# A hybrid mLSTM/attention layer: the second modulation's weight pieces, summed in the first piece's own buffer and loaded three ahead

## The chip, the cores and the metric

The kernel runs on 1 core of one Trainium2 chip. The metric is the device time of one execution in microseconds (us), the median of several runs. The engines are named as the profile names them: PE (TensorE; PEld are its weight loads), DVE (VectorE), ACT (ScalarE), POOL (GpSimd) and SP (SyncE). SP issues nearly all DMAs here, one after the other: a DMA that has to wait for something holds up those behind it in SP's queue.

## The reference

One layer over 1024 latent and 256 context tokens of width 1024. The part that the change touches is the modulation: a matrix product of the activated conditioning vector `c` with `w_ada`, whose six results shift, scale and gate the two halves of the layer.

```python
sh_a, sc_a, g_a, sh_f, sc_f, g_f = jnp.split(
    (jax.nn.silu(c) @ w_ada[l] + b_ada[l])[:, None, :], 6, axis=-1)
...
hx = modulate(rmsnorm(x, norm_mix[l]), sh_a, sc_a)
qm, km, vm, om, gates_x, qa, ka, va = project_tokens(hx, w_in[l], qk_conv_w[l], qk_conv_b[l], gate_b[l])
hm, _, _ = mlstm_bidirectional(qm, km, vm, gates_x, st_f, st_b, True)
...
x = x + g_a * (jnp.concatenate([y_m, y_a], axis=-1) @ w_out[l])
x = x + g_f * conv_glu(modulate(rmsnorm(x, norm_ffn[l]), sh_f, sc_f),
                       w_up[l], ffn_conv_w[l], ffn_conv_b[l], w_down[l])
return rmsnorm(x, final_norm)
```

`sh_a` and `sc_a` are needed at once (the first modulation). The other four, `g_a`, `sh_f`, `sc_f` and `g_f`, are needed only behind the mixer: they are the second modulation. `project_tokens` has four mLSTM heads and an attention part; `mlstm_bidirectional` runs a recurrence over chunks of tokens in both directions.

## The kernel before

The kernel is one long program. It norms and modulates the tokens, projects them head by head, runs the mLSTM heads and the attention, the output projection and the channel mixer. The loop that matters here is the one over the four mLSTM heads: in pass `h` the recurrence of head `h` (`mlstm(h, ...)`, about 30 steps, each up to a `yield`) runs beside the projections of head `h + 1` (`dense(h + 1, ...)`: L580 and L588 are products of keys and queries, L307 to L309 those of values and output gates). These passes are called head 0, 1 and 2 here, by `h`; in head 3 the attention's query projections (`qgen`) run beside the recurrence. After each step of the recurrence a budget (`RATE`) lets so much of the projections go. The engines' order in these passes is the order in which the code is written, for PE, DVE, ACT, POOL and SP alike (the manual schedule).

The second modulation is spread over heads 0 to 2 as a third strand, `ada_second`. Its matrix lies in DRAM as `w_ada2`, two halves of 32 pieces; a piece is 128 x 512 floats, 256 KB, and a tile of 2 KB in each partition. One call of the generator (`next(ada, 0)` behind nearly every step of the recurrence) does one piece: DVE multiplies it by a column of `silu(c)` (`c4`). The first piece of a half is written so into the accumulator `acc` (L830, a tensor_scalar), the 31 others are added to it (L832, a scalar_tensor_tensor). `total` (L816, L818) then sums over partitions on PE and adds the bias. For the first half `total` stands behind the fourth piece of the second half, for the second half at the end. The result `ada2` is transposed and goes to DRAM (`row_d`) through the tile `arw`, and is read again in the later stages.

The pieces lie in the pool `ap2`, opened with two buffers for each name: two tiles `w2` for pieces and two tiles `acc`. Two loads (L811) go out before the first piece; after piece `i` is used, piece `i + 2` is loaded, into the buffer that piece `i` leaves. The load is written behind the multiply-add that frees its buffer, so SP waits there for DVE.

Other names that the prediction uses: L152 loads a projection weight `wr` in two transfers of 512 KB, L156 (ACT) and L157 (DVE) split it into two parts. L549, L551, L554 and L556 are the short convolution and its activation on `kT`, by DVE, DVE, ACT and DVE. L600 and L601 copy a value block from PSUM to `va` and `ym` on ACT; PE's next block waits for that room. L690 is the backward state of the recurrence, L704 a gate on `ym`, L619 a copy of the context's values, L725 the decay matrix `ee` times scores, all on DVE. L722 are PE's scores, L736 PE's products with `ee`. L541 loads `tri`, a mask, L647 `ee`, L848 a block of attention keys `kb`.

Of the kernel before, what the change touches and what calls it, by code (L numbers as in the profile page):

```python
# [9 lines left out]
F32 = mybir.dt.float32  # L10
# [8 lines left out]
P = 128  # L19
# [59 lines left out]
def build(tc, I, out, dbg=None):  # L79
    nc = tc.nc  # L80
# [15 lines left out]
    def spc(n, i=0, w=1):  # L96
        a = SP[n][0] + i
        return sp[:, a:a + w]
# [45 lines left out]
    def load_split(src, w, rawf=None, split=True, alloc=True, now=range(2)):  # L144
        room = lambda: [st.tile([P, KT, XW], F32R, name=n, tag=n)[:].rearrange("p a b -> p (a b)")[:, :KT * w]
                        .rearrange("p (k f) -> p k f", k=KT) for n in ("wh", "wl")]
        hi, lo = room() if alloc else (None, None)
        raws = {}

        def load(q):  # L150
            raws[q] = rawf() if rawf else sr.tile([P, 4, XW], F32, name="wr", tag="wr")
            nc.sync.dma_start(raws[q][:, :, :w], src[:, 4 * q:4 * q + 4, :])  # L152

        def cut(q):
            ks, raw = slice(4 * q, 4 * q + 4), raws[q]
            S.copy(hi[:, ks, :w], raw[:, :, :w])  # L156
            V.tensor_tensor(out=lo[:, ks, :w], in0=raw[:, :, :w], in1=hi[:, ks, :w].bitcast(F32), op=ALU.subtract)  # L157

        if split:
            for q in range(2):  # L160
                load(q)
                cut(q)
            return hi, lo
        for q in now:
            load(q)

        def rest(qs=range(2)):
            nonlocal hi, lo
            if hi is None:
                hi, lo = room()  # L170
            for q in qs:
                cut(q)
            return hi, lo
        rest.load = load
        return rest
# [279 lines left out]
    qk = mstk.enter_context(tc.tile_pool(name="qk", bufs=2))  # L455
    tp = mstk.enter_context(tc.tile_pool(name="tp", bufs=2))
    astk = ExitStack()
    ap2 = astk.enter_context(tc.tile_pool(name="ap2", bufs=2))

    def g80(name, dt=F32):  # L460
        return gp.tile([P, 2, NCH, H], dt, name=name)
# [96 lines left out]
    def heads():  # L558
        return (qk.tile([P, NCH * P], F32, name="kT", tag="kT"), qk.tile([P, SEQ], F32, name="qT", tag="qT"),
                qk.tile([P, NCH, DH + 1], F32, name="va", tag="va"))  # L560
# [242 lines left out]
    def ada_second():  # L803
        R4 = 4 * KT
        pieces = [(n, r) for n in range(2) for r in range(R4)]
        tiles = {}

        def load(i):
            if i < len(pieces):
                tiles[i] = ap2.tile([P, 512], F32, name="w2", tag="w2")  # L810
                nc.sync.dma_start(tiles[i][:], I["w_ada2"][pieces[i]])  # L811

        def total(n, acc):
            pq = pl.tile([P, 512], F32, name="pq", tag="l")
            for j in range(4):
                T.matmul(pq[:, 4 * j:4 * j + 4], acc[:, j * P:(j + 1) * P], spc("c", 0, 4), start=True, stop=True)  # L816
            v = lambda a: a.rearrange("p (q j) -> p q j", q=4)
            V.tensor_tensor(out=v(ada2[:, 16 * n:16 * n + 16]), in0=pq[:, 0:16].rearrange("p (j q) -> p q j", q=4),  # L818
                            in1=v(spc("b2", 16 * n, 16)), op=ALU.add)

        load(0)
        load(1)
        yield
        prev = None
        for i, (n, r) in enumerate(pieces):
            w2 = tiles.pop(i)
            cr = spc("c4", r)
            if r == 0:
                acc = ap2.tile([P, 512], F32, name="acc", tag="acc")
                V.tensor_scalar(out=acc[:], in0=w2[:], scalar1=cr, scalar2=None, op0=ALU.mult)  # L830
            else:
                V.scalar_tensor_tensor(out=acc[:], in0=w2[:], scalar=cr, in1=acc[:], op0=ALU.mult, op1=ALU.add)  # L832
            load(i + 2)
            if r == 3 and n:
                total(n - 1, prev)
            prev = acc if r == R4 - 1 else prev
            yield
        yield
        yield
        total(1, prev)  # L840

    def row(i):
        return row_d[8 * i:8 * i + 8, :].rearrange("(o a) b -> o (a b)", o=1).broadcast_to([P, D])
# [90 lines left out]
    def qgen():  # L934
        for t, (i, b) in enumerate(qseq):
# [11 lines left out]
            if t == 2 * NL - 2:  # L947
                load_q(0)

    ada = ada_second()  # L950
    ahead_load = lambda h, i: load_split(I["w_h"][h, i] if h < H else I["w_q"][i], 256, split=False, alloc=False)

# [19 lines left out]
    for h in range(H):  # L972
        order_ = {mybir.EngineType.PE}
        if h + 1 < H:
            order_ |= {mybir.EngineType.DVE, mybir.EngineType.Activation, mybir.EngineType.Pool, mybir.EngineType.SP}
        else:
            wq = [wkq]
            late = lambda: wq.append(load_split(I["w_q"][1], 256, lambda: pq.tile([P, 4, 256], F32, name="wr", tag="rga")))
            for _ in ada:
                pass  # L980
            V.scalar_tensor_tensor(out=ada2[:, 16:24], in0=ada2[:, 16:24], scalar=1.0, in1=spc("nffn", 0, KT), op0=ALU.add, op1=ALU.mult)
            prw = pl.tile([P, 512], F32, name="prw", tag="l")
            T.transpose(prw[:32, 0:P], ada2[:], ident[:])
            arw = ap2.tile([P, 512], F32, name="arw", tag="w2")
            V.tensor_copy(arw[:32, 0:P], prw[:32, 0:P])
            nc.sync.dma_start(row_d[:], arw[:32, 0:P])
            cstk.close()
            astk.close()
            pq = rstk.enter_context(tc.tile_pool(name="pq", bufs=1, side="right"))
        wvo = []  # L990
        nh = heads() if h + 1 < H else None
        debt = 0.0
        with tc.manual_schedule(engines=order_):
            dn = dense(h + 1, wkq, wvo, *nh) if nh else qgen()
            rate = RATE if nh else RATE3
            for n, _ in enumerate(mlstm(h, *cur)):
                if nh is None and n == LW3:
                    late()
                    rga = pq.tile([P, D], F32, name="rga", tag="rga")
                    nc.sync.dma_start(rga[:], row(0))  # L1000
                if nh and n in (2, LW):
                    w = wnext((n // LW,))
                    if n == LW:
                        wvo.append(w)
                        wnext = ahead_load(h + 2, 0)
                elif nh and n in (24, 27):
                    wkq = wnext((n // 27,))
                    if n == 27 and h + 2 < H:
                        wnext = ahead_load(h + 2, 1)
                elif nh and n >= 3 and n != 15:  # L1010
                    next(ada, 0)
                debt += rate * (1 + (n == 0))
                while debt > 0:
                    w = next(dn, None)
                    if w is None:
                        break
                    debt -= w
            if nh is None:
                mstk.close()
                plk.close()  # L1020
                pl = pT = pa_.enter_context(tc.tile_pool(name="pT", bufs=2, space=PSUM))
                pO = pa_.enter_context(tc.tile_pool(name="pO", bufs=1, space=PSUM))
                pU = pa_.enter_context(tc.tile_pool(name="pU", bufs=1, space=PSUM))
                wm = rstk.enter_context(tc.tile_pool(name="wm", bufs=1, side="right"))
                kT2 = [wm.tile([P, KVH, NCH * P], F32R, name=f"kT2{i}") for i in range(2)]
                vv = wm.tile([P, NCH, KVH, P], F32R, name="vv")
                S.activation(vv[:, 0, 0, 0:1], eps_t[:], AF.Exp)
                kgens += [kprep(c) for c in range(NCH)]
                loads += [lambda: load_vv(0), lambda: load_vv(1)]
                wosteps += WOS  # L1030
            for _ in dn:
                pass
        cur = nh
# [23 lines left out]
    class Wout:  # L1057
# [8 lines left out]
        def load(self):  # L1066
            b = self.b
            self.xb = t3.tile([P, D], F32, name="x2", tag="x2") if self.attn else x2t()
            if self.attn:
                xs[b] = self.xb[:]  # L1070
            nc.sync.dma_start(self.xb[:], x2_d[b][:] if self.attn else I["x"][b * P:(b + 1) * P, :])
# [196 lines left out]
    for t in range(n + 2):  # L1268
# [3 lines left out]
        if t in WOT:  # L1272
            k = 4 + WOT.index(t)
# [215 lines left out]
    for i, b in enumerate(order):  # L1489
        prev = order[i - 1] if i else None  # L1490
# [71 lines left out]
    f = ExitStack()  # L1562
# [20 lines left out]
    def wsplit_h(R, n):  # L1583
# [5 lines left out]
        def lo():  # L1589
# [41 lines left out]
                                                                    tag={"a": "a", "f": "b", "b": "b"}.get(n, "c"))  # L1631
# [383 lines left out]
    for t, (p, ps, fresh) in enumerate(products):  # L2015
        for j in range(NP):
# [12 lines left out]
            if n - 1 in sums:  # L2029
                k = sums[n - 1]  # L2030
                m = len(PAIRS[k])
                add(V, b11[k][:, 0:m], b22[k][:, 0:m], b11[k][:, 0:m])
            if n + 2 in raws:
                q, k = steps[n + 2]
# [10 lines left out]
            if n in sums:  # L2045
                k = sums[n]
# [125 lines left out]
```

## Time and profile before

| what | value |
|---|---|
| median of 3 runs | 1273.13 us (1272.91 to 1273.3) |
| the profiled execution | 1274.79 us |
| its span in the profile | 1273.0 us |
| granted TensorE clock, mean | 0.997 |
| loads of pieces (L811) | 64, of 256 KB each, 81.6 to 305.6 us |
| multiply-adds into `acc` (L832) | 62, 746 ns median |
| head 0, 1, 2 begin with L580 at | 125.77, 190.85 and 257.93 us |

The span is shorter than the time of the execution by what lies around it. An engine's busy time is the time in which one of its instructions ran. In the list of waits an engine's idle time is put down to the instruction that ended it; SPq is SP's queue of DMAs. In the timeline an instruction's idle time before it stands in brackets, with what ended it, and neighbours of one line are merged (x2 are two).

### The profile page before, as it was taken

What the parts mean: (1) busy time and instruction counts of PE and PEld (TensorE: products, weight loads), DVE (VectorE), ACT (ScalarE), POOL (GpSimd) and SP (SyncE); (2) the same over time, 40 slices, a digit from 0 to 9 for tenths busy, and PEclk for the clock granted to TensorE, in tenths of its full rate; (3) what the DMA queues carried; (4) which work ended last, traced back from release to release, by engine and by line L of the source; (5) the groups of instructions that cost most, each with busy time, mean ns of one, the idle gap of its engine ahead of it and who ended that gap; (6) DMA issues with size and microseconds to landing.
All of it is one profiled execution on the core that took longest, in us unless ns stands there. A gap on an engine that the chain in (4) does not pass through costs nothing.

```text
span 1273.0 us, 19254 instructions
## 1 busy us (share of the span) xinstructions
PE 1238.7 (97%) x7047; PEld 1062.6 (83%) x7047; DVE 974.5 (77%) x1691; ACT 638.0 (50%) x1309; POOL 188.0 (15%) x162
## 2 busy tenths in 40 slices
PE   6999999999999999999999999999999999999997
PEld 4799998989898888887877888888888888788886
DVE  4873687868787888788987877777777776867887
ACT  6732556464765877775844333333333333434435
POOL 1200000000000443221002331232231232001000
PEclk9999999999999999999999999999999999999999
DMA  9541544453255333104413322333322337975553
GB/s 356 186 125 35 142 129 145 117 170 92 79 166 171 133 117 117 51 33 136 146 50 116 115 100 92 108 108 108 108 99 91 108 119 268 342 255 179 196 194 135
DMA packets 90560, 176.17 MB, mean 138 GB/s; under 512 B 12954, under 2 KB 29538, under 8 KB 90466
## 3 DMA queue, kind: packets, MB, share of 16 engines
q1 hardware_dynamic: 90178, 174.15, 40.6%
q8 instruction: 56, 0.92, 0.3%
q10 hardware_dynamic: 288, 0.79, 0.2%
q14 instruction: 38, 0.31, 0.1%
HBM read 136.58 MB, written 38.33 MB: 137 GB/s over the span
## 4 chain that ended last, share of the span: by engine, by line
PE 76%; DVE 9%; ACT 6%; DMA 5%; issue 2%; POOL 1%; SPq 0%; ACTq 0%; DVEq 0%; POOLq 0%
PE pd L2009 14%; PE pa L1471 8%; PE pc L1471 8%; PE pp L588 7%; PE pe L1471 4%; PE pd L1471 4%; PE pb L1471 4%; PE u L1177 3%; PE pt L1154 2%; PE pv L307 2%; PE pv L309 2%; PE pv L308 2%; PE po L307 1%; PE po L309 1%; PE po L308 1%
## 5 line engine op out<-in xcount | busy, mean ns | idle before, releaser
L1587 ACT CAST wh<-Rb 128x1024 fp32r<-128x1024 f32 (+1 forms) x63 | 56.8, 904 | 144.4 <-PE pd L1471 77.3
L2009 PE MATMUL pd<-dh,al 128*128 128x512 f32 x296 | 115.4, 390 | 0.9 <-DVE al L1352 0.9
L2009 PE MATMUL pd<-dl,ah 128*128 128x512 f32 x296 | 115.3, 389 | 0.0
L2009 PE MATMUL pd<-dh,ah 128*128 128x512 f32 x296 | 115.1, 389 | 0.0
L1471 PE MATMUL pc<-hB,wh 128*128 128x512 f32 x344 | 105.6, 389 | 0.0
L1471 PE MATMUL pa<-hB,wh 128*128 128x512 f32 x336 | 103.7, 390 | 0.3 <-ACT sn L1668 0.2
L1193 DVE TENSOR_TENSOR wl<-Rb,wh 128x1024 fp32r<-128x1024 f32 (+1 forms) x63 | 65.8, 1046 | 39.2 <-ACT wh L1587 38.7
L1704 POOL TENSOR_TENSOR tt<-vt,tt 128x512 f32<-128x512 f32 x22 | 29.6, 1343 | 368.5 <-ACT tt L1698 368.5
L588 PE MATMUL pp<-hl,wh 128*128 128x512 f32 x256 | 79.3, 405 | 0.0
L307 PE MATMUL pv<-wh,hl 128*128 128x256 f32 x256 | 76.1, 297 | 0.8 <-ACT ym L601 0.8
L1471 PEld LDWEIGHTS pc<-hB,wh 128*128 128x128 f32 x344 | 64.6, 188 | 13.4
L1471 PEld LDWEIGHTS pa<-hB,wh 128*128 128x128 f32 x336 | 62.9, 188 | 14.1 <-ACT sn L1668 1.1
L309 PE MATMUL pv<-wh,hl 128*128 128x256 f32 x256 | 72.3, 283 | 0.0
L308 PE MATMUL pv<-wl,hl 128*128 128x256 f32 x256 | 72.3, 282 | 0.0
L2009 PEld LDWEIGHTS pd<-dh,al 128*128 128x128 f32 x296 | 55.6, 188 | 13.2 <-DVE al L1352 1.6
L1471 PE MATMUL pc<-hB,wl 128*128 128x512 f32 x172 | 66.4, 389 | 0.0
L1471 PE MATMUL pa<-hB,wl 128*128 128x512 f32 x168 | 65.4, 389 | 0.0
L2009 PEld LDWEIGHTS pd<-dl,ah 128*128 128x128 f32 x296 | 55.6, 188 | 11.7 <-DVE dl L1352 0.3
L2009 PEld LDWEIGHTS pd<-dh,ah 128*128 128x128 f32 x296 | 55.6, 188 | 11.6
L1161 ACT CAST ph<-pt 128x512 fp32r<-128x512 f32 (+1 forms) x88 | 46.2, 525 | 28.2 <-PE pt L1154 28.0
L1471 PE MATMUL pb<-hB,wh 128*128 128x512 f32 x176 | 54.0, 390 | 0.6 <-ACT hB L1443 0.6
L1131 DVE TENSOR_REDUCE nm<-sps 128x1 f32<-128x641 f32 (+1 forms) x64 | 50.3, 786 | 4.9 <-PE sps L1127 3.5
(1080 smaller groups left out, 3702.9 us busy)
## 6 DMA issues: line engine op xcount, KB each, us to landing
w<-in_w_ada_dram SPq DMA_DIRECT2D x64, 256.0 KB, 2.7
br<-in_w_down_dram SPq DMA_DIRECT2D x25, 512.0 KB, 5.2
ar<-act_s SPq DMA_DIRECT2D x44, 256.0 KB, 3.1
Ra<-in_w_up_dram SPq DMA_DIRECT2D x21, 512.0 KB, 3.6
Rb<-in_w_up_dram SPq DMA_DIRECT2D x21, 512.0 KB, 3.6
act_a<-tt SPq DMA_DIRECT2D x33, 256.0 KB, 2.0
act_s<-tt SPq DMA_DIRECT2D x33, 256.0 KB, 2.0
wr<-in_w_h_dram SPq DMA_DIRECT2D x16, 512.0 KB, 4.4
```

The source lines that it names most:

```text
L307: T.matmul(ps, st_hi, mv_hi, start=first, stop=False)
L308: T.matmul(ps, st_hi, mv_lo, start=False, stop=False)
L309: T.matmul(ps, st_lo, mv_hi, start=False, stop=last)
L588: T.matmul(pp[:, 512 * n:512 * n + 512], wkq[sw][:, kt, cs], hl[n][part][:, kt, :], start=kt == 0 and sw + part == 0, stop=kt == KT - 1 an ...
L1131: V.tensor_reduce(out=self.nm[:, j:j + 1], in_=self.sv[j], axis=AX.X, op=ALU.max, negate=True)
L1161: S.copy(self.ph[i][:, :w], self.pt[i][:, :w])
L1177: T.matmul(self.u[:], vv[:, c, self.g], part[i][:, kk * 2 * P:(kk + 1) * 2 * P], start=kb + m == 0, stop=kb == last and m == 1)
L1193: sub = lambda e, o, x, y: e.tensor_tensor(out=o, in0=x, in1=y, op=ALU.subtract)
L1471: T.matmul(ps[:, cols], wt[sw][:, j, kt * P:kt * P + P], hB[part][:, blk, kt, cols], start=first and n == 0, stop=last and n == len(seq) - ...
L1587: S.copy(wt[0][:], src)
L1704: G.tensor_tensor(out=self.tt[:, h2_], in0=self.vt[:], in1=self.tt[:, h2_], op=ALU.mult)
L2009: T.matmul(ps[:], ac[sa][:, js], w[sw], start=first and n == 0, stop=last and n == 2, skip_group_check=not fresh)
```

## The change

The pool `ap2` has one buffer for each name, and there are four names, `w20` to `w23`: four tiles as before, of the same size, but any of them can take a piece. A list `rooms` says which are free. Four loads go out before the first piece. The first piece of a half is multiplied in its own tile, which then is the accumulator of that half; it isn't given back until the half is summed. Every other piece gives its tile back when it has been added. So three tiles take pieces while one half is in work, and the load that follows a multiply-add is the piece three steps ahead. At the turn of the halves both accumulators hold a tile, and two take pieces until `total` of the first half has read its accumulator; its tile is then given back, and the load into it waits for PE. `arw` uses the name `w20`.

```diff
-    ap2 = astk.enter_context(tc.tile_pool(name="ap2", bufs=2))
+    ap2 = astk.enter_context(tc.tile_pool(name="ap2", bufs=1))
...
-        tiles = {}
-
-        def load(i):
-            if i < len(pieces):
-                tiles[i] = ap2.tile([P, 512], F32, name="w2", tag="w2")
-                nc.sync.dma_start(tiles[i][:], I["w_ada2"][pieces[i]])
+        tiles, rooms = {}, list(range(4))
+
+        def load():
+            while rooms and todo_:
+                k, i = rooms.pop(0), todo_.pop(0)
+                tiles[i] = k, ap2.tile([P, 512], F32, name="w2", tag=f"w2{k}")
+                nc.sync.dma_start(tiles[i][1][:], I["w_ada2"][pieces[i]])
+
+        todo_ = list(range(len(pieces)))
...
-        load(0)
-        load(1)
+        load()
         yield
         prev = None
         for i, (n, r) in enumerate(pieces):
-            w2 = tiles.pop(i)
+            k, w2 = tiles.pop(i)
             cr = spc("c4", r)
             if r == 0:
-                acc = ap2.tile([P, 512], F32, name="acc", tag="acc")
+                acc, held_ = w2, k
                 V.tensor_scalar(out=acc[:], in0=w2[:], scalar1=cr, scalar2=None, op0=ALU.mult)
             else:
                 V.scalar_tensor_tensor(out=acc[:], in0=w2[:], scalar=cr, in1=acc[:], op0=ALU.mult, op1=ALU.add)
-            load(i + 2)
+                rooms.append(k)
             if r == 3 and n:
                 total(n - 1, prev)
-            prev = acc if r == R4 - 1 else prev
+                rooms.append(done)
+            load()
+            if r == R4 - 1:
+                prev, done = acc, held_
             yield
...
-            arw = ap2.tile([P, 512], F32, name="arw", tag="w2")
+            arw = ap2.tile([P, 512], F32, name="arw", tag="w20")
```

On PE, DVE, ACT and POOL every instruction keeps its place; on SP only loads of pieces move. In the changed program L811 is L812, L816 is L819, L830 and L832 are L832 and L834, and what stands behind is 5 lines further down. The names of tiles carry a number; `w_1427` is the first piece's tile.

The start of SP's queue, ahead of head 0 and at its first steps (line, what is written from where, shape, times). Before:

```order
L811 DMA w_1427<-in_w_ada_dram 128x512
L811 DMA w_1429<-in_w_ada_dram 128x512
L541 DMA tri<-in_cst_dram 128x256
L152 DMA wr<-in_w_h_dram 128x4x256 x2
L539 DMA m_d<-rr 40x256
L647 DMA ee<-m_d 128x2x256 x3
L811 DMA w_1563<-in_w_ada_dram 128x512
L647 DMA ee<-m_d 128x2x256
L811 DMA w_1582<-in_w_ada_dram 128x512
L152 DMA wr<-in_w_h_dram 128x4x256 x2
```

With the change:

```order
L812 DMA w_1427<-in_w_ada_dram 128x512
L812 DMA w_1429<-in_w_ada_dram 128x512
L812 DMA w_1431<-in_w_ada_dram 128x512
L812 DMA w_1433<-in_w_ada_dram 128x512
L541 DMA tri<-in_cst_dram 128x256
L152 DMA wr<-in_w_h_dram 128x4x256 x2
L539 DMA m_d<-rr 40x256
L647 DMA ee<-m_d 128x2x256 x4
L812 DMA w_1583<-in_w_ada_dram 128x512
L152 DMA wr<-in_w_h_dram 128x4x256 x2
```

Two loads have moved to the front, and the load of the first step is gone, since the first piece keeps its tile.

SP's queue in head 2, about the weights that are loaded for the attention's queries. Before:

```order
L811 DMA w_3125<-in_w_ada_dram 128x512
L647 DMA ee<-m_d 128x2x256
L811 DMA w_3145<-in_w_ada_dram 128x512
L152 DMA wr<-in_w_q_dram 128x4x256 x2
L811 DMA w_3193<-in_w_ada_dram 128x512
L811 DMA w_3212<-in_w_ada_dram 128x512
L848 DMA kb<-kv_d 128x2x64 x2
```

With the change:

```order
L812 DMA w_3125<-in_w_ada_dram 128x512
L647 DMA ee<-m_d 128x2x256
L812 DMA w_3145<-in_w_ada_dram 128x512
L152 DMA wr<-in_w_q_dram 128x4x256 x2
L812 DMA w_3193<-in_w_ada_dram 128x512
L812 DMA w_3212<-in_w_ada_dram 128x512
L853 DMA kb<-kv_d 128x2x64 x2
```

The rows stand alike; what has changed is which step of DVE reads which of these tiles. DVE's order at the same place, before:

```order
L832 SCALAR_TENSOR_TENSOR acc<-w_3145,sp,acc 128x512
L605 MEMSET va 128x10
L690 SCALAR_TENSOR_TENSOR cbk<-cbk,gd,pn 128x129
L787 SCALAR_TENSOR_TENSOR ym<-hid,hss,ym 128x128
L663 TENSOR_TENSOR ee<-ee,tri 128x256
L832 SCALAR_TENSOR_TENSOR acc<-w_3193,sp,acc 128x512
L549 SCALAR_TENSOR_TENSOR kT<-pp,sp,kT 128x1023
L551 SCALAR_TENSOR_TENSOR kT<-pp,sp,kT 128x1023
```

With the change (`w_2505` is the tile of the second half's first piece):

```order
L834 SCALAR_TENSOR_TENSOR w_2505<-w_3125,sp,w_2505 128x512
L605 MEMSET va 128x10
L690 SCALAR_TENSOR_TENSOR cbk<-cbk,gd,pn 128x129
L787 SCALAR_TENSOR_TENSOR ym<-hid,hss,ym 128x128
L663 TENSOR_TENSOR ee<-ee,tri 128x256
L834 SCALAR_TENSOR_TENSOR w_2505<-w_3145,sp,w_2505 128x512
L549 SCALAR_TENSOR_TENSOR kT<-pp,sp,kT 128x1023
L551 SCALAR_TENSOR_TENSOR kT<-pp,sp,kT 128x1023
```

The step ahead of L549 reads the tile that is loaded ahead of `wr` (w_3145), where before it read the one loaded behind it (w_3193).

## Prediction

> **What bounds the kernel now.** I read the profile's page first, then the waits, then the chain of waits and the timeline in the stretch where the pieces are used (126 to 326 us), and last the busy time by windows.
>
> ```profile
> span 1273.0 us, 19254 instructions
> ...
> PE 1238.7 (97%) x7047; PEld 1062.6 (83%) x7047; DVE 974.5 (77%) x1691; ACT 638.0 (50%) x1309; POOL 188.0 (15%) x162
> ...
> PE 76%; DVE 9%; ACT 6%; DMA 5%; issue 2%; POOL 1%; SPq 0%; ACTq 0%; DVEq 0%; POOLq 0%
> ```
>
> PE is busy for 97% of the span. So a wait on another engine has a price only where PE runs out of work because of it. The pieces are read by DVE, and DVE's waits for them are these (the waits of the stretch 90 to 330: who waits, for whom, sum in us, times, longest):
>
> ```profile
> DVE acc L832 <- DMA w<-in_w_ada_dram: 8.7, 6, 2.9
> ...
> DVE acc L830 <- DMA w<-in_w_ada_dram: 1.5, 1, 1.5
> ...
> PE pv L307 <- ACT ym L601: 0.8, 2, 0.6
> ...
> PE pn L710 <- DVE cbk L690: 0.7, 1, 0.7
> ```
>
> DVE stands still 8.7 + 1.5 = 10.2 us in 7 waits for a piece. That is not the price: in the same stretch PE waits for ACT and DVE only 0.8 + 0.7 us. What PE loses in all is found by comparing like with like. The heads 0, 1 and 2 run the same PE work behind each other, and the chain of waits shows the same two landmarks in each: the context product L580 that opens a head's projections, and the first L588 group behind the first use of `ee` (start us, us, what). L816 is PE's sum of a finished half, which head 0 hasn't.
>
> ```profile
> 125.77 2.88 PE pc__1491 L580 x24
> 157.81 1.39 PE pp L588 x6
> ...
> 190.85 2.88 PE pc__2263 L580 x24
> 224.02 1.38 PE pp L588 x6
> 229.49 0.79 PE pq L816 x8
> 257.93 2.88 PE pc__3051 L580 x24
> 292.50 1.38 PE pp L588 x6
> ```
>
> From landmark to landmark: head 0 takes 157.81 - 125.77 = 32.04 us, head 1 224.02 - 190.85 = 33.17, head 2 292.50 - 257.93 = 34.57. Head 1 loses 1.13 us and head 2 2.53 us, **3.66 us** together; L816 lies behind the landmark. Which of the seven waits is behind them is read from DVE's and ACT's timeline (start, us, engine, line; in brackets the idle time before and what ended it):
>
> ```profile
> 211.91 0.75 DVE L832 SCALAR_TENSOR_TENSOR acc<-w,sp,acc 128x512 f32<-128x512 f32 x1 [1.49 <-DMA w<-in_w_ada_dram]
> 215.26 1.03 ACT L554 ACTIVATE pp<-kT 128x1024 f32<-128x1024 f32 x1 [3.44 <-DVE kT L551]
> ...
> 280.38 0.75 DVE L832 SCALAR_TENSOR_TENSOR acc<-w,sp,acc 128x512 f32<-128x512 f32 x1 [2.86 <-DMA w<-in_w_ada_dram]
> 283.56 0.34 DVE L690 SCALAR_TENSOR_TENSOR cbk<-cbk,gd,pn 128x129 f32<-128x129 f32 x1
> 283.74 1.03 ACT L554 ACTIVATE pp<-kT 128x1024 f32<-128x1024 f32 x1 [4.79 <-DVE kT L551]
> ```
>
> One wait in each of the two heads, 1.49 and 2.86 us, stands just ahead of the convolution (L549, L551). ACT waits for L551 and copies `ym` (L601) only after it; PE waits for that copy, and in head 2 for L690 too. The other waits fall in head 0 or behind the second landmark, where PE has work queued.
>
> **The change part by part.** *The wait that goes.* Why these two pieces come late is in SP's timeline; first one row of head 1, then head 2, and behind them the landing times of all 64 loads of pieces:
>
> ```profile
> 203.94 0.34 SPq L811 DMA_DIRECT2D w<-in_w_ada_dram  x1
> ...
> 271.04 0.34 SPq L811 DMA_DIRECT2D w<-in_w_ada_dram  x1
> 271.43 2.25 SPq L152 DMA_DIRECT2D wr<-in_w_q_dram  x2
> ...
> 274.83 2.19 SPq L811 DMA_DIRECT2D w<-in_w_ada_dram  x2
> ```
>
> ```profile
> DMA to landing us min/median/max: 2.4/2.7/5.5
> ```
>
> A piece is issued when the piece two steps before it has been used. The late one (w_3193) was issued at 274.83, behind two halves of the next weights (`wr`, 512 KB each), and landed just ahead of its use at 280.38: some 5.5 us, the longest of all 64, against a median of 2.7. In the changed program the queue stands the same, but the load ahead of `wr` is already the one that this step reads. Issued at 271.04 and landed 2.4 to 5.5 us later, it is there by 273.4 to 276.5; DVE is ready for it at 280.38 - 2.86 = 277.52. So even the slowest landing seen leaves 1.0 us, and the wait goes whole. In head 1 the load ahead of such a pair goes out at 203.94, is there by 209.4 at the latest, and DVE is ready at 211.91 - 1.49 = 210.42.
>
> *What is late next.* The piece behind `wr` is now read one step later, at L832 behind L704. Before, that step stood at 285.55; without the wait it stands at 282.69:
>
> ```profile
> 285.55 0.75 DVE L832 SCALAR_TENSOR_TENSOR acc<-w,sp,acc 128x512 f32<-128x512 f32 x1
> ```
>
> The piece issued at 274.83 landed by 280.38, so 2.3 us are left. And DVE, so freed, stands where it stood in head 0, which cost PE nothing. Two of its instructions in the three heads, L704 and the copy L619 for which PE's L722 waits:
>
> ```profile
> 149.59 1.22 DVE L704 SCALAR_TENSOR_TENSOR ym<-ym,rw 128x1024 f32<-128x1024 f32 x1
> 153.78 0.41 DVE L619 COPY va<-pt 128x256 f32<-128x256 f32 x1
> ...
> 215.94 1.22 DVE L704 SCALAR_TENSOR_TENSOR ym<-ym,rw 128x1024 f32<-128x1024 f32 x1
> 220.39 0.41 DVE L619 COPY va<-pt 128x256 f32<-128x256 f32 x1
> ...
> 284.42 1.22 DVE L704 SCALAR_TENSOR_TENSOR ym<-ym,rw 128x1024 f32<-128x1024 f32 x1
> 288.87 0.41 DVE L619 COPY va<-pt 128x256 f32<-128x256 f32 x1
> ```
>
> Counted from each head's L580, L704 stands at 23.82, 25.09 and 26.49 us; less the waits 23.82, 23.60 and 23.63. L619 stands at 28.01, 29.54 and 30.94; less the waits 28.01, 28.05 and 28.08. So heads 1 and 2 come to head 0's schedule within 0.1 us, and I take the whole difference of PE: 1.13 + 2.53 = 3.66 us.
>
> *How PE's loss is counted.* The windows show idle PE directly (stretch, length, PE busy first):
>
> ```profile
> 190.60:257.60 67.00, 66.67 (x474) 61.67 (x473) 51.51 (x124) 37.05 (x105) 0.00 (x0) 1.00 0.46 138
> 257.60:326.00 68.40, 66.96 (x473) 61.70 (x473) 49.17 (x120) 37.26 (x106) 0.00 (x0) 1.00 0.37 110
> ```
>
> By them PE is idle 67.00 - 66.67 = 0.33 and 68.40 - 66.96 = 1.44 us, 1.77 together, half of 3.66. I take 3.66: start times of the same work are measured, while a record that overlaps the next covers part of a stall. The Trainium skill, Perfetto Trace Analysis, Identifying the Most-Contended Engine, says that matmul busy time is a poor measure of what is left in PE, because of pipelining; by that rule the 1.77 is a floor. The granted clock in these rows is 1.00, so no slower clock is in either sum.
>
> *What the change adds.* Two more loads go out at the start, behind the two at 81.56:
>
> ```profile
> 81.56 0.91 SPq L811 DMA_DIRECT2D w<-in_w_ada_dram  x2
> 93.06 0.33 SPq L541 DMA_DIRECT2D tri<-in_cst_dram  x1
> ```
>
> They take another 0.91 us of SP's queue, in which nothing is issued from 82.5 to 93.06; the cost is nothing, and without that cover it would be 0.91 us of a queue whose next DMA waits for PE anyway. The first piece of a half is scaled in place. That form isn't in the trace; its neighbours are the same form into another tile (484 ns) and the in-place multiply-add (746 ns):
>
> ```profile
> L832 DVE SCALAR_TENSOR_TENSOR acc<-w,sp,acc x62: 730/746/753, 136.2 to 309.0; 128x512 f32<-128x512 f32 x62
> L830 DVE TENSOR_SCALAR acc<-w,sp x2: 479/484/489, 134.8 to 224.8; 128x512 f32<-128x512 f32 x2
> ```
>
> I take 484; at worst it is 2 x 0.27 = 0.54 us of DVE, at two places where PE doesn't wait for it. At the turn of the halves both accumulators hold a buffer, and for two steps loads run two ahead as before. Then the load into the first accumulator's buffer waits for L816 on PE, and SP's queue behind it with it. PE began L816 at 229.49, ahead of the multiply-add at 230.67 that frees the other buffer of that step; I take nothing.
>
> ```profile
> 230.67 0.73 DVE L832 SCALAR_TENSOR_TENSOR acc<-w,sp,acc 128x512 f32<-128x512 f32 x1
> ...
> 237.22 0.74 DVE L832 SCALAR_TENSOR_TENSOR acc<-w,sp,acc 128x512 f32<-128x512 f32 x1
> ```
>
> **The sum.** The profiled execution took 1274.79 us (span 1273.0, and 1.79 around it): 1274.79 - 3.66 = 1271.13. It lies 1.66 above the median of the runs, 1273.13. The median less the same 3.66 is **1269.5 us**.
>
> **The rivals.** *Only the idle rows count* (1.77 us): 1273.13 - 1.77 = 1271.4. For it: nothing else in PE's rows is idle. Against it: the landmarks.
>
> *The wait moves one step.* If the piece behind `wr` lands after 282.69, 2.3 us later than it did, DVE waits there instead, ahead of the same L619 and L722. If head 2 keeps its loss and only head 1 is healed, the gain is 1.13: 1272.0. For it: the pair still stands in front. The Trainium skill, DMA: Bandwidth & Descriptors, Queues, rings and completion order, says that each DMA engine takes the descriptors of a ring in order; by that rule the late landing stays and only its reader moves. The trace agrees as far as the 5.5 us of that piece go.
>
> *Given back later, or the change doesn't do what it says.* PE comes 3.66 us earlier into the rest, and something that doesn't move with it (a landing, another engine) takes it back: 1273.1. Against it: from 292 us on every transfer is issued behind work that moves along.
>
> *Slower: the load that waits for L816 holds SP.* The piece that it brings is read at 237.22 and needs 2.7 us, so SP must be free by 234.5, 4.2 us after L816's end at 230.28. A longer hold delays DVE one for one, and beyond the 0.3 us that a wait had free (2.86 - 2.53) PE too; the gain is used up from a hold of 4.2 + 0.3 + 3.66 = 8.2 us on. If SP were held as long as its longest wait for DVE in this stretch,
>
> ```profile
> SPq L152 <- DVE wl L157: 20.6, 1, 20.6
> ```
>
> PE would lose 20.6 - 4.5 = 16.1 us, less the gain 12.4: 1285.6. Against it: L816 is in PE's order at a fixed place, ahead of what frees the other buffer.
>
> **How the numbers follow.** A measurement of this kernel tells about 0.2% from no change, 2.55 us: faster means below 1270.6. Forecast 1269.5: 0.70, its own range 1268.7 to 1270.4 (all of 3.66 and some of head 3's waits, or 0.9 less). Idle rows 1271.4: 0.08. Wait moved 1272.0: 0.08. Given back 1273.1: 0.10. Slower: 0.04. Up to 1272.0 the cases hold 0.86, so the range is 1268.7 to 1272.0. Faster 0.70, same 0.08 + 0.08 + 0.10 = 0.26, slower 0.04.
>
> **What would show it.** In the changed profile DVE's waits for `w` should be almost gone (below 1 us of 10.2), the landmarks 32.0 to 32.2 us apart in all three heads, PE's waits for L601 and L690 gone, and the rest behind 292 us as long as before. The forecast is wrong if DVE waits at the step behind L704, if SP waits for PE at L816's load, or if the landmarks close up and the span doesn't.

## The result and the profile after

The changed kernel takes 1269.11 us (median of 7 runs, 1268.51 to 1271.46), the kernel before in the same comparison 1273.13 us (7 runs, 1271.55 to 1274.38): a ratio of 0.9976, 95% interval 0.9967 to 0.9985 (the quotient of the two medians is a little lower, 0.9968). A second comparison, below, gave 0.9969 (0.9956 to 0.9981). The change is worth 3 to 4 us.

The profiled execution of the changed kernel took 1268.82 us. The head of its page, and the chain that ended last:

```profile
span 1267.0 us, 19250 instructions
...
PE 1234.5 (97%) x7047; PEld 1059.8 (84%) x7047; DVE 974.1 (77%) x1691; ACT 639.0 (50%) x1309; POOL 187.7 (15%) x162
...
PE 80%; DVE 7%; ACT 5%; DMA 4%; issue 2%; SPq 1%; POOL 1%; ACTq 0%; DVEq 0%; POOLq 0%
```

PE bounds it as before, with a larger part of the chain. From the waits of the stretch 90 to 330 us (who waits, for whom, sum in us, times, longest):

```profile
ACT pp L554 <- DVE kT L551: 5.4, 4, 1.9
...
DVE w L834 <- DMA w<-in_w_ada_dram: 0.8, 3, 0.4
...
PE pn L680 <- ACT kwf L659: 0.2, 1, 0.2
```

DVE's waits for pieces have gone from 10.2 us in 7 to 0.8 us in 3. PE's waits for L601 and L690 are gone; what is left to PE up to 326 us, where the prediction counted 0.8 + 0.7 us, is 0.2 us. In the chain of waits the two landmarks of each head now read (start us, us, what):

```profile
125.27 2.88 PE pc__1495 L580 x24
...
157.30 1.39 PE pp L588 x6
...
190.34 2.88 PE pc__2264 L580 x24
...
222.35 1.38 PE pp L588 x6
...
256.28 2.88 PE pc__3051 L580 x24
...
288.33 1.39 PE pp L588 x6
```

The distances are 32.03, 32.01 and 32.05 us; before they were 32.04, 33.17 and 34.57. Heads 1 and 2 now take what head 0 took, to within 0.02 us.

The same place in head 2, by SP's timeline and then DVE's:

```profile
269.39 0.35 SPq L812 DMA_DIRECT2D w<-in_w_ada_dram  x1
269.78 2.26 SPq L152 DMA_DIRECT2D wr<-in_w_q_dram  x2
273.19 2.19 SPq L812 DMA_DIRECT2D w<-in_w_ada_dram  x2
```

```profile
275.79 0.75 DVE L834 SCALAR_TENSOR_TENSOR w<-w,sp,w 128x512 f32<-128x512 f32 x1
276.45 1.29 DVE L549 SCALAR_TENSOR_TENSOR kT<-pp,sp,kT 128x1023 f32<-128x1023 f32 x1
277.77 1.28 DVE L551 SCALAR_TENSOR_TENSOR kT<-pp,sp,kT 128x1023 f32<-128x1023 f32 x1
...
279.82 1.22 DVE L704 SCALAR_TENSOR_TENSOR ym<-ym,rw 128x1024 f32<-128x1024 f32 x1
280.96 0.75 DVE L834 SCALAR_TENSOR_TENSOR w<-w,sp,w 128x512 f32<-128x512 f32 x1
```

The rows have no bracket, so DVE didn't stand still. The step ahead of L549 reads the piece issued at 269.39. The load behind `wr` still took 5.50 us to land (at 278.69, by its record), but it is read at 280.96, 2.27 us later.

### The profile page after: what moved, and what is told of

Read it like the earlier page. It is cut to its first block, busy times and chain, and to the rows that moved or that the text cites. A ratio compares the mean times of both kernels' runs of the same rounds, so it can differ in the third digit from the quotient of the medians.

```text
span 1267.0 us, 19250 instructions
## 1 busy us (share of the span) xinstructions
PE 1234.5 (97%) x7047; PEld 1059.8 (84%) x7047; DVE 974.1 (77%) x1691; ACT 639.0 (50%) x1309; POOL 187.7 (15%) x162
## 4 chain that ended last, share of the span: by engine, by line
PE 80%; DVE 7%; ACT 5%; DMA 4%; issue 2%; SPq 1%; POOL 1%; ACTq 0%; DVEq 0%; POOLq 0%
PE pd L2014 14%; PE pa L1476 8%; PE pc L1476 8%; PE pp L588 7%; PE pe L1476 4%; PE pd L1476 4%; PE pb L1476 4%; PE u L1182 3%; PE pv L307 2%; PE pv L309 2%; PE pv L308 2%; PE pt L1159 2%; PE po L307 1%; PE px L309 1%; PE po L309 1%
```

## The experiments

The pieces are counted from 0 to 63. Two matter: piece 27, read ahead of L549 in head 1, and piece 50 (`w_3193` in the order), read there in head 2. "Loss" below is the time from landmark to landmark less 32.03 us.

### The kernel as changed, once more

No edit.

> The changed kernel once more. Theory (PE's loss in heads 1 and 2 is gone, nothing else moved): 3.66 us below the kernel before in its runs, ratio 0.9971, and in the profile heads 0, 1 and 2 within 0.1 us of each other on PE from L580 to the first L588 group behind `ee` (32.0 us each). Rival (the other 2.3 us by which the first profile of the changed kernel was shorter, 0.5 ahead of head 0 and 1.8 behind head 2, belong to the change): 5.5 to 6 us below, ratio 0.9955, and PE's start of head 0 again at 125.0 and not 125.5.

1268.89 us (6 runs, 1268.14 to 1271.02) against 1273.25 (23 runs, 1271.41 to 1275.47) on another chip, a ratio of 0.9969 (0.9956 to 0.9981). Heads 32.03, 32.01 and 32.05 us. The gain is there again.

### Four tiles and the sum in place, but two ahead

```diff
-        def load():
-            while rooms and todo_:
+        def load(end=2):
+            while rooms and todo_ and todo_[0] < end:
...
-            load()
+            load(i + (4 if i + 3 in () else 3))
```

The brackets behind `in` are empty here, so the limit is `i + 3`: behind step `i` the last piece that may be loaded is `i + 2`.

> The changed kernel with its loads held back to two ahead; first piece still summed in place, four tiles. Theory (only the third step of lead counts): the time of the kernel before, 1273.1, ratio 1.000; DVE again waits some 1.5 and 2.9 us just ahead of L549 in heads 1 and 2, and PE loses 1.1 and 2.5 us there. Rival (summing in place, or the other layout of the tiles, is what helps): 1269.5, ratio 0.997.

1270.19 us (10 runs, 1269.27 to 1270.92), ratio 0.9977 (0.9968 to 0.9986). That was not what I expected of a kernel that loads two ahead. SP's timeline in head 2, and DVE's wait for piece 50:

```profile
268.29 0.34 SPq L812 DMA_DIRECT2D w<-in_w_ada_dram  x1
268.68 4.17 SPq L152 DMA_DIRECT2D wr<-in_w_q_dram  x2
272.89 3.28 SPq L812 DMA_DIRECT2D w<-in_w_ada_dram  x3
```

```profile
277.61 0.75 DVE L834 SCALAR_TENSOR_TENSOR w<-w,sp,w 128x512 f32<-128x512 f32 x1 [0.92 <-DMA w<-in_w_ada_dram]
```

Piece 50 is still behind `wr`, but both go out earlier. With a fourth tile to spare the oldest free one takes the load, and its reader is long done, so SP doesn't wait for the multiply-add of its own step. Head 2 began at 257.11 here, so piece 50 was issued 15.78 us into it; before it was 274.83 - 257.93 = 16.90. The wait fell from 2.86 to 0.92 us, and the losses of heads 1 and 2 from 1.13 and 2.53 to 0.54 and 0.59 us. My edit had not made the kernel that I meant: a lead counted in pieces is not a lead in time.

### The same, with piece 50 alone one step earlier

```diff
-            load(i + (4 if i + 3 in () else 3))
+            load(i + (4 if i + 3 in (50,) else 3))
```

> Loads two ahead as in the run before, but the one piece that is read ahead of L549 in head 2 is loaded a step earlier, ahead of the pair of wr. Theory (two single late pieces, 1.13 us of PE for that in head 1 and 2.53 for that in head 2): head 2 as short as head 0 on PE (32.0 us), head 1 still 33.2; time 1273.1 - 2.5 = 1270.6, ratio 0.998. Rival (the waits of all pieces add up, 10.2 us in 7 waits): a seventh to a quarter of the gain, 1272.2 to 1272.6, ratio 0.9993 or more; or the wait moves to the next piece, and head 2 keeps 34.6.

1270.68 us (10 runs, 1269.05 to 1272.39), ratio 0.9978 (0.9969 to 0.9987). By the landmarks head 2 is whole (32.04 us) and head 1 keeps 0.45 us of loss. The two medians don't tell this kernel from the one above, since little was left to heal.

### The kernel before, with `wr` issued one step later

Two tiles for pieces as before; only SP's order changes: the two `wr` transfers of these places go out behind the next piece.

```diff
                     if n == LW:
                         wvo.append(w)
-                        wnext = ahead_load(h + 2, 0)
...
                     next(ada, 0)
+                    if n == LW + 1:
+                        wnext = ahead_load(h + 2, 0)
```

> The kernel before, loads two ahead into two tiles, accumulators apart, with one edit: the pair of wr that stands ahead of the late piece in heads 0 to 2 is issued one step of the recurrence later, behind that piece's load. Theory (the pair in front makes the piece late, 5.5 us against 2.7): the piece issued at about 274.8 lands by 277.5, when DVE is ready for it at 277.5; both waits shrink to 0.3 us or less, heads 1 and 2 are within 0.2 us of head 0 on PE, and the time is that of the changed kernel, 1269.5, ratio 0.997. Rival (two ahead is too little lead with or without the pair): PE still loses over 1.5 us in heads 1 and 2 together, 1271 or more.

1269.55 us (8 runs, 1269.07 to 1270.14), ratio 0.9974 (0.9964 to 0.9984): the changed kernel's gain to within the intervals, with the old buffers. Piece 50 was issued 16.89 us into head 2 (273.07 - 256.18), as before (16.90), and landed 2.59 us later by its record, not 5.46. SP's timeline in head 2, then DVE's waits for pieces in all three heads:

```profile
269.28 4.14 SPq L811 DMA_DIRECT2D w<-in_w_ada_dram  x2
273.51 0.95 SPq L152 DMA_DIRECT2D wr<-in_w_q_dram  x2
274.92 1.95 SPq L811 DMA_DIRECT2D w<-in_w_ada_dram  x2
```

```profile
DVE acc L832 <- DMA w<-in_w_ada_dram: 4.8, 7, 1.5
...
DVE acc L830 <- DMA w<-in_w_ada_dram: 1.6, 1, 1.6
```

DVE still waits 6.4 us for pieces, against 10.2 before, but at most 0.13 us at a time ahead of L549 in heads 1 and 2. Here the wait does move one step: pieces 28 and 51, now behind `wr`, hold DVE for 0.44 and 0.37 us just behind L704, and heads 1 and 2 lose 0.31 and 0.12 us. Head 1 so misses the 0.2 us that was expected. So the old buffers give the gain too, and the sum of DVE's waits doesn't set it. What counts is which load stands behind `wr` in the queue and what DVE has to do behind its reader.

### Two ahead in earnest, and then one or two pieces earlier

To let SP wait again for the step's own multiply-add, the newest free tile takes the load:

```diff
-                k, i = rooms.pop(0), todo_.pop(0)
+                k, i = rooms.pop(), todo_.pop(0)
...
-                rooms.append(done)
+                rooms.insert(0, done)
```

Together with the limit of two ahead this is the first kernel here; the second also issues piece 50 one step earlier (`if i + 3 in (50,)`), and the third pieces 27 and 50. All three sum in place and have four tiles.

> The changed kernel (first piece summed in place, four tiles), each load held back to two ahead and put into the tile that the last multiply-add has just left, as in the kernel before; one tile lies idle. In the run two_ahead the load went into a tile that had been free for a step, so SP did not wait for the multiply-add and issued 1.3 to 1.9 us earlier than before. Theory (a piece is late by its time of issue): the late pieces are issued about 4.7 us behind the step before L549's as in the kernel before, DVE waits 1.5 and 2.9 us there, PE loses 1.1 us in head 1 and 2.5 in head 2, time 1273.2, ratio 1.000. Rival (summing in place, or one tile more, helps by itself): 1270.2 as two_ahead, ratio 0.998.

> strict_two, but the piece that is read ahead of L549 in head 2 is loaded one step earlier, into the idle tile. Theory (two single pieces): head 2 as short as head 0 on PE within 0.1 us, head 1 still 1.1 longer; 2.5 us below strict_two, 1270.7, ratio 0.998. Rival (the late landing moves to the next piece, which is now behind the pair of wr): DVE waits over 1 us behind L704 and head 2 keeps 1 us or more of its loss, 1272 or more.

> strict_two with both such pieces, in head 1 and head 2, loaded one step earlier; all 62 others stay two ahead. Theory: PE's loss in heads 1 and 2 is gone (within 0.1 us of head 0), although DVE still waits some 6 us for other pieces; the time of the changed kernel, 1269.5, ratio 0.997. Rival (the other five waits have a part in the gain): half of the gain or less, 1271.4 or more.

Against 1272.97 us (23 runs, 1271.2 to 1274.93):

| kernel | median (runs) | ratio, 95% interval | loss of heads 0, 1, 2 |
|---|---|---|---|
| two ahead in earnest | 1273.39 (11) | 1.0003 (0.9994 to 1.0012) | 0.18, 1.59, 2.41 |
| and piece 50 earlier | 1271.95 (11) | 0.9989 (0.9980 to 0.9998) | 0.09, 1.35, 0.01 |
| and piece 27 too | 1270.38 (7) | 0.9976 (0.9966 to 0.9987) | 0.87, 0.00, 0.01 |

The first line says that the sum in place and the fourth tile are worth nothing by themselves: this kernel has both, and the time and the losses of before. From line to line head 2 and then head 1 heals when its own piece is moved, and no sooner. The medians follow less closely: with piece 50 earlier 1270.7 was expected, and 1271.95 is nearer to the rival's 1272. The rival's own signs are absent all the same, since head 2 is whole and DVE doesn't wait behind L704. SP's timeline and the landmarks of the third kernel in head 1, where the waits left over are seen to cost nothing:

```profile
204.92 0.82 SPq L812 DMA_DIRECT2D w<-in_w_ada_dram  x2
205.84 1.72 SPq L152 DMA_DIRECT2D wr<-in_w_h_dram  x2
```

```profile
191.82 2.88 PE pc__2262 L580 x24
...
223.83 1.38 PE pp L588 x6
```

```profile
224.17 0.49 DVE L832 TENSOR_SCALAR w<-w,sp 128x512 f32<-128x512 f32 x1 [1.52 <-DMA w<-in_w_ada_dram]
227.01 0.75 DVE L834 SCALAR_TENSOR_TENSOR w<-w,sp,w 128x512 f32<-128x512 f32 x1 [1.76 <-DMA w<-in_w_ada_dram]
```

Piece 27 stands ahead of `wr` now (it is the second of the two loads merged in a row), and 223.83 - 191.82 = 32.01 us. DVE stands still 1.52 and 1.76 us just behind the second landmark and the next head is no later for it: head 2 begins 65.94 us behind head 1 here (at 257.76), as in the first profile of the changed kernel, where DVE waits 0.4 us there.

Head 0 of this kernel loses 0.87 us, at a place that no edit touched. Piece 7 is late, and it is read ahead of L725, whose result PE's L736 needs (DVE's rows, then PE's):

```profile
155.98 0.75 DVE L834 SCALAR_TENSOR_TENSOR w<-w,sp,w 128x512 f32<-128x512 f32 x1 [1.11 <-DMA w<-in_w_ada_dram]
157.57 0.42 DVE L725 SCALAR_TENSOR_TENSOR ee<-pe,ee 128x256 f32<-128x256 f32 x1
```

```profile
158.04 0.71 PE L736 MATMUL pi<-va,ee 128*128 128x129 f32 x4 [0.28 <-DVE ee L725]
```

### Both kernels profiled again

The first two profiles differ by 6.0 us of span, more than the medians or the landmarks. Five more profiles, without an edit, say what of that belongs to the change.

> The kernel before, for a second profile of it. Theory (what lies ahead of head 0 and behind head 2 varies from run to run): heads 1 and 2 lose 1.1 and 2.5 us on PE again, and from the first landmark of head 3's start to the end PE takes 1 us or more less than in the first profile. Rival (the change also shortens the later stages by some 2 us): the second profile agrees with the first to 0.5 us in each stretch behind head 2.

> A third profile of the kernel before. Theory (the two late pieces land 3.9 to 5.5 us after issue as the queue of transfers happens to stand, so PE's loss varies from run to run): heads 1 and 2 lose 1.9 to 3.7 us together. If the step of 0.8 us near 580 us, which six profiles of other kernels show against the first, is a matter of the run, it can show here too; if it comes with the four tiles, it can't.

> A fourth profile of the kernel before: as for the third, 1.9 to 3.7 us lost in heads 1 and 2, and the step near 580 us present or not.

> A third profile of the changed kernel. Theory: no loss on PE in heads 1 and 2 (below 0.1 us), whatever the landings. The step of 0.8 us near 580 us: present, if it comes with the change; absent in some, if it is a matter of the run.

> A fourth profile of the changed kernel: as for the third, no loss in heads 1 and 2, and the step near 580 us present or not.

The profiles of both kernels and of `wr` later (us; "changed, 2" is from the second comparison; "rest" is from the second landmark of head 2 to the end of the span). This table counts from the first record of each landmark, some 0.24 us ahead of the chain's row, so its distances can differ by 0.01 us from those above:

| profile | heads 0, 1, 2 | loss | rest | span |
|---|---|---|---|---|
| before, 1 | 32.03, 33.17, 34.57 | 3.68 | 980.7 | 1273.0 |
| before, 2 | 32.17, 33.30, 33.03 | 2.41 | 980.2 | 1271.2 |
| before, 3 | 32.03, 33.54, 34.54 | 4.02 | 980.2 | 1272.7 |
| before, 4 | 32.53, 33.48, 33.48 | 3.40 | 980.8 | 1272.8 |
| changed, 1 | 32.03, 32.01, 32.04 | 0.0 | 978.9 | 1267.0 |
| changed, 2 | 32.03, 32.01, 32.05 | 0.0 | 981.1 | 1269.2 |
| changed, 3 | 32.03, 32.01, 32.04 | 0.0 | 979.7 | 1268.0 |
| changed, 4 | 32.03, 32.01, 32.04 | 0.0 | 981.7 | 1270.4 |
| `wr` later | 32.03, 32.34, 32.15 | 0.4 | 980.1 | 1268.2 |

The loss is 2.4 to 4.0 us before, 3.4 in the mean, and nothing in any of the four profiles of the changed kernel. The rest is 980.5 us in the mean before and 980.4 after, and varies by 2.8 us within the changed kernel alone. So the 2.3 us that the first pair of profiles differ by beyond the landmarks can't be put down to the change.

Two expectations were missed. In the second profile of before the two heads lost 1.27 and 1.00 us, not 1.1 and 2.5, and its rest was only 0.5 us shorter than the first's, where 1 us or more was expected. In the third they lost 4.02 us together, above the 3.7 expected.

The step near 580 us, which the expectations speak of, is a drop of the granted clock. The windows of the first profile of before and of the changed kernel at about the same work (stretch, length, PE busy first; the granted clock is the third number from the end):

```profile
579.00:582.30 3.30, 3.30 (x14) 2.90 (x13) 1.18 (x3) 1.11 (x3) 0.00 (x0) 0.50 0.54 212
```

```profile
573.80:576.50 2.70, 2.61 (x16) 2.30 (x17) 1.04 (x4) 1.58 (x4) 0.00 (x0) 1.00 0.77 285
```

For 3.4 us PE ran at half its clock there. Its lag on the changed kernel grows by 1.6 us between 575 and 590 us. All four profiles of before have this drop, and so have `wr` later and two ahead in earnest with piece 50 earlier. None of the four of the changed kernel has it, nor any other kernel here. In turn the second and fourth profile of the changed kernel lose 2.2 to 2.4 us between 590 and 650 us, which the other two don't. No run shows what sets off either. The gain doesn't hang on the drop as far as one profile of each kernel tells: `wr` later has it and gains, two ahead in earnest hasn't and gains nothing.

Why the loss varies is seen in DVE's row for piece 50 in the second profile of before:

```profile
279.15 0.75 DVE L832 SCALAR_TENSOR_TENSOR acc<-w,sp,acc 128x512 f32<-128x512 f32 x1 [1.32 <-DMA w<-in_w_ada_dram]
```

It was issued at 275.14 and landed in 3.9 us, not 5.5, and head 2 lost 1.00 us in this profile (33.03 - 32.03), not 2.54.

## Why the prediction was right, point by point

- **The two waits that cost.** Of seven waits it picked two and priced the other five at nothing. The experiments on single pieces show this: heads 1 and 2 heal each with its own piece, and 1.5 us of waiting behind the landmark costs nothing. But the reason was only half given. A third wait of the seven stands ahead of L549 too, in head 0:

```profile
145.82 0.75 DVE L832 SCALAR_TENSOR_TENSOR acc<-w,sp,acc 128x512 f32<-128x512 f32 x1 [1.29 <-DMA w<-in_w_ada_dram]
146.49 1.28 DVE L549 SCALAR_TENSOR_TENSOR kT<-pp,sp,kT 128x1023 f32<-128x1023 f32 x1
```

  It cost nothing, nor did 1.59 and 1.70 us at this place in the two kernels that load two ahead with the oldest free tile. The way by which the other two reach PE is in the chain of before (head 2):

```profile
274.83 5.46 DMA w<-in_w_ada_dram
...
280.38 0.75 DVE acc L832
281.13 1.21 DVE kT L549
...
288.95 0.34 DVE va L619
...
289.34 0.49 PE pe L722 x2
```

  By this chain the copy L619, for which PE's L722 waits, decides, and not the copy of `ym` on ACT (L601), which the prediction named with it. Without waits L619 comes 27.97 and 27.99 us behind L580 in heads 1 and 2 of the changed kernel, but 26.63 us in head 0. So head 0 had 1.3 us more room. It was luck that head 0, with a wait in it, could serve as the measure of the others: the prediction took its 28.01 us for a schedule without waits. Head 0 has a weak place of its own besides, piece 7 ahead of L725: it cost 0.5 us in the fourth profile of before and 0.87 us in the kernel with pieces 27 and 50 moved. In the changed kernel head 0 lost nothing in four profiles.
- **The cause.** The piece behind `wr` comes late. Moving `wr` alone, with the old buffers, gave 0.9974, and the same load, issued as late in the head but ahead of `wr`, landed in 2.59 us in place of 5.46. That leaves nothing measurable for the buffers themselves to explain.
- **The size.** 3.66 us was this profile's value; the mean of four is 3.4. By the ratios the two comparisons gave 3.1 and 3.9 us, with intervals of 1.9 to 4.2 and 2.4 to 5.6 us. All agree. That the median lies within 0.4 us of the forecast is partly luck: one profile of before could as well have said 2.4 or 4.0.
- **Start times or idle rows.** The windows of the changed kernel, cut at the same work to within 0.2 us (stretch, length, PE busy first):

```profile
190.10:256.00 65.90, 65.90 (x474) 61.47 (x473) 51.40 (x124) 37.25 (x105) 0.00 (x0) 1.00 0.46 139
256.00:322.00 66.00, 66.00 (x475) 61.53 (x474) 49.14 (x121) 37.42 (x106) 0.00 (x0) 1.00 0.38 110
```

  The stretches are 1.10 and 2.40 us shorter than before, 3.50 together. Idle rows make up 1.77 of it; the other 1.73 us was time that PE counted as busy (66.67 to 65.90 and 66.96 to 66.00), for the same matmuls but one or two records. So the 1.77 was a floor here. The Trainium skill, Perfetto Trace Analysis, Identifying the Most-Contended Engine, says only that matmul busy time is a poor measure because pipelined instructions look smaller in the trace. Which way the idle rows err was the prediction's own step, and these windows bear it out.
- **The wait moves one step.** It didn't. The late landing stayed with the piece behind `wr` (5.50 us), but its new reader left 2.27 us, where 2.3 was forecast. That agrees with what the prediction took from the Trainium skill, DMA: Bandwidth & Descriptors, Queues, rings and completion order: each DMA engine takes the descriptors of a ring in order.
- **Given back later.** Not in the mean: the rest is as long in four profiles against four. The prediction saw neither the drop of the clock in before nor the 2.2 to 2.4 us that two profiles of the changed kernel lose behind 590 us; in the mean they nearly cancel.
- **SP held for L816.** It wasn't. The load that waits for PE's sum went out at 230.17, right behind its neighbour at 229.79, and PE's sum had ended at 228.63.
- **The added parts.** The first piece in place took 483 and 485 ns, against the 484 taken. The first kernel that loads two ahead in earnest shows that form and tiles have no price of their own (1.0003).

What the prediction didn't settle is a small earlier start: the changed kernel's head 0 begins 0.3 us sooner in the mean of four profiles, with spreads that overlap (125.00 to 125.64 against 125.43 to 125.55, from the first record). No run tells whether the change does that; `wr` later, with the old buffers, begins at 124.59, and two ahead in earnest, with the new ones, at 125.58.

## What to carry to other kernels

Price a wait by the start times of like work on the engine that bounds, from a stretch with the wait to one without it; idle rows of that engine gave half here, and the sum of the waiting engine's time nearly three times as much. See first that the stretch without the wait has none: head 0 had one, which cost nothing only because there was more room. When a small load comes late, look first at what stands ahead of it in its queue: putting the large load behind the small urgent one bought here what a deeper buffer bought. And count a buffer's lead from the load's issue to its use: a spare tile that lets the queue run without waiting for the last reader had two thirds of the effect of a piece more in flight (a loss of 1.13 us in place of 3.4).

## What the runs showed of the hardware

The same load, at the same place in the queue behind two transfers of 512 KB, landed in 3.9, 4.4, 5.4 and 5.5 us in four profiles of one program, against a median of 2.7 us for the pieces whose landing is on record (55 of 64), and in 2.59 us when it was issued as late but ahead of the two. So one profile can size such a stall wrongly by 1 us: the four give 2.4, 3.4, 3.7 and 4.0 us.

A wait of DVE ahead of L549 in heads 1 and 2 cost PE less than its length by 0.32 to 0.36 us, in all 14 cases of 0.81 to 2.86 us on record: 1.49 us cost 1.13, 2.86 cost 2.53, 0.92 cost 0.59 and 0.81 cost 0.45. That much slack stood between DVE's convolution and PE, so waits of 0.3 us and less there can be left alone.

The granted clock of PE can drop to 0.5 for 3.4 us in the middle of a program and cost it 1.6 us, in all four profiles of one kernel and in none of four of another that does the same work (3.30 us of it stand at 0.50 in the window shown above).
